# Plain feed-forward blocks with tokens stationary and results turned by DMA, three attention units per layer turned by DMA, and additions placed behind the scaled rows, in a two-layer decoder trunk

## The chip, the cores and the metric

The kernel runs on one core of a Trainium2 chip. The metric is the device time of one execution in microseconds (us), the median of several runs. The profile is one execution recorded by the hardware profiler. Its engines are TensorE (PE; its weight loads are listed apart as PEld), VectorE (DVE), ScalarE (ACT), GpSimd (POOL) and SyncE (SP), which here only issues DMA transfers.

## The reference

The model is a decoder trunk of two layers on 512 tokens of width 1024, all in float32. Each layer is a feed-forward network (2816 hidden columns), a mixing stage with attention and a short convolution side by side, and a second feed-forward network. Cut to what matters here:

```python
def swiglu(h, w_gate, w_up, w_down):
    return (jax.nn.silu(h @ w_gate) * (h @ w_up)) @ w_down
...
    for l in range(DEPTH):
        x = x + 0.5 * swiglu(rms_norm(x, ffn1_norm[l]), ffn1_wg[l], ffn1_wu[l], ffn1_wd[l])

        h = rms_norm(x, mix_norm[l])
        z = h @ w_in[l]
...
        attn_out = sliding_window_attention(q, k, v, attn_sink[l])
        conv_out = short_conv(z[..., V_END:CB_END], z[..., CB_END:CC_END],
                              z[..., CC_END:CH_END], conv_w[l])
        x = x + jnp.concatenate([attn_out, conv_out], axis=-1) @ w_out[l]

        x = x + 0.5 * swiglu(rms_norm(x, ffn2_norm[l]), ffn2_wg[l], ffn2_wu[l], ffn2_wd[l])
    return rms_norm(x, final_norm)
```

Attention has 8 query heads and 2 key-value heads of 64 dimensions, a window of 128 tokens, a linear position bias and a learned sink in the softmax.

## The kernel before

**Numbers in two parts.** Every product is made of three matmuls: each operand is split into a high part (rounded to the fast float type of TensorE) and the low rest, and high x high, low x high and high x low are summed. For a weight tile the high part is a ScalarE cast (`wh`, L205) and the low part a VectorE subtraction (`wl`, L206). `need_raw` loads the raw tile by a DMA from SP's queue (L189) or adds another matrix to it by a DMA from POOL's queue (L200). `take_split` hands a product its tile and has the later ones split ahead. `plan()` fixes the order of all weight tiles, and so the order of the loads on SP and of the casts and subtractions.

**Feed-forward.** Most hidden columns go through blocks that use a seven-product scheme for 2x2 blocks of matrices (`winograd2`, L1081, and `share`, L896, whose matmuls are all in `stream`, L885): tokens are the stationary operand there, 512 weight columns move. Some blocks of 256 hidden columns are "plain", computed directly. The first network of the first layer has two, in another function; the other three networks begin with one, in `plain_halves` (L985). There a weight tile of 128 columns is stationary and the tokens move, in two halves of 256: three tiles in `halves` (L324), the fourth in its own loop (L1010). Since the result has hidden columns on the partitions, it can serve at once as stationary operand of the down-projection. ScalarE applies Silu (L998), VectorE multiplies (L990), and `split` makes the two parts of the result.

**The norm in front.** Class `Norm` sums squares (`sq`, L593) as rows of x are finished; when the four rows of a token half are there, `stage` computes the root (`v`, `r`, `y`) and the scaled rows `xn` (L625). `pull` has TensorE turn two of them (`xt`, L649, eight transposes); casts and subtractions (L658, L659) make the operands `fb` or `hh`. The first half's transposes stand inside the last product of the stage before, the second half's inside the plain block: after 48 and after 60 of its 256-column matmuls. `share(after=norm)` is that stage before in three places (the first network of layer 0 and both output products of the mixing stage). Its accumulators are added to x on VectorE (L924); in its seven steps, `x_m` is step 5 and `z_m`, the last, step 6.

**Turning by DMA, as it is already used.** In `winograd2` the result has tokens on the partitions and must be turned. float32 rows are taken apart into two planes of 16 bits (`apart`, L1098, ScalarE), each plane is sent through a DMA transpose (`send`, L1104, SP's queue), and the turned planes are joined again (`join`, L1158, ScalarE). These steps are put into later blocks by a clock of ticks, two for a weight tile's product.

**Attention.** `mix` (L1360) runs the products with `w_in` and, in between, eight units (4 token blocks x 2 key-value heads; unit number 4g + n). Step by step `attend` (L1499) calls `scores` (matmuls L1435, L1436; exponentials L1456; scaling L1464), `turn` (4 transposes for the first token block, 8 for the others, L1472; casts `ph` L1475, subtractions `pl` L1476) and `values` (L1487, L1488, the product `o`; copy `ol` L1490; addition L1493). The tables SCORES_AT, TURN_AT, VALUES_AT give the steps. Behind each step `go_on` asks for the next weight split.

**Order of work.** A scheduler orders each engine's program; `tc.issue_after(...)` puts an instruction behind a given one in it, and `by_hand` to `by_itself` keeps TensorE's order as written.

## Time and profile before

| | us |
|---|---|
| median of 3 runs | 1652.32 |
| lowest and highest | 1650.25, 1654.33 |
| profiled execution, its own time | 1650.43 |
| span of the profiled execution | 1648.7 |

The granted clock of TensorE is 0.999 of full speed over the span. A row of the chain of waits reads: start, duration, engine, tile, line, number of instructions; a row of a group: busy time and mean duration, then the idle time of the engine just before those instructions and what ended it.

Feed-forward blocks behind norms stand at 502.8 to 527.7, at 828.7 to 853.5 and at 1317.7 to 1342.5 us; attention of layer 0 lies at 375 to 460 us, that of layer 1 some 815 us later. The plain block at 828.7 stands behind a down-projection, the two others behind an output product of the mixing stage.

### The profile page before, as it was taken

Reading aid. Unit: us, or ns where it says so; the run is one execution under the profiler, and the core shown is the slowest. Engines: PE = TensorE matmul, PEld = TensorE weight load, DVE = VectorE, ACT = ScalarE, POOL = GpSimd, SP = SyncE. Lnnn points to the kernel's source line nnn. Section 1 sums busy time; section 2 is a strip of 40 time slices with the busy share of each in tenths; the row PEclk is TensorE's granted clock in tenths of the full one; section 3 lists DMA queues with packets and bytes.
Section 4 is the critical chain, followed back from the end, with each engine's and each line's share of the span. In section 5 each row is a group of like instructions: output and inputs, shape, how many; then the busy total and the mean of one; then the engine's idle time right before and its main releaser. Section 6 shows DMA issues by size and latency. Waiting matters only on the chain.

```text
span 1648.7 us, 21650 instructions
## 1 busy us (share of the span) xinstructions
PE 1637.2 (99%) x7912; PEld 1376.7 (84%) x7912; DVE 1303.5 (79%) x1712; ACT 1089.3 (66%) x1527; POOL 193.0 (12%) x172
## 2 busy tenths in 40 slices
PE   9999999999999999999999999999999999999998
PEld 6888898888889888888898888888988798888886
DVE  7987779867799777798797677896587987767895
ACT  7457777556567567786565777864565765777864
POOL 0011111100111111112001111110002101111111
PEclk9999999999999999999999999999999999999999
DMA  9369999931494778899837889996126946899991
GB/s 256 89 192 225 225 217 257 213 90 52 129 211 108 204 197 212 217 229 251 222 84 185 207 216 220 237 245 189 52 65 155 226 108 168 220 213 231 227 260 71
DMA packets 273791, 303.97 MB, mean 184 GB/s; under 512 B 89332, under 2 KB 157972, under 8 KB 273684
## 3 DMA queue, kind: packets, MB, share of 16 engines
q1 hardware_dynamic: 231156, 223.27, 45.9%
q0 software_dynamic: 41824, 78.65, 28.1%
q8 instruction: 62, 1.02, 0.2%
q10 hardware_dynamic: 704, 0.66, 0.1%
q14 instruction: 45, 0.37, 0.1%
HBM read 263.74 MB, written 2.10 MB: 161 GB/s over the span
## 4 chain that ended last, share of the span: by engine, by line
PE 96%; DVE 2%; ACT 1%; DMA 1%; issue 0%; SPq 0%; ACTq 0%; DVEq 0%
PE x L885 25%; PE y L885 13%; PE x_s L885 10%; PE w L885 6%; PE y_s L885 5%; PE acc L324 5%; PE acc L297 4%; PE acc L298 4%; PE acc L300 4%; PE down L347 3%; PE w_s L885 3%; PE up L1010 1%; PE xt L649 1%; PE y_m L885 1%; PE x_m L885 1%; PE acc L783 1%
## 5 line engine op out<-in xcount | busy, mean ns | idle before, releaser
L206 DVE TENSOR_TENSOR wl<-raw,wh 128x1024 fp32r<-128x1024 f32 (+1 forms) x493 | 599.2, 1220 | 232.2 <-ACT wh L205 231.5
L205 ACT CAST wh<-raw 128x1024 fp32r<-128x1024 f32 (+1 forms) x493 | 512.9, 1044 | 363.8 <-PE acc L298 54.0
L885 PE MATMUL x<-wh,fb 128*128 128x512 f32 x608 | 187.1, 389 | 0.0
L885 PE MATMUL y<-wh,ft 128*128 128x512 f32 x608 | 187.1, 389 | 0.0
L885 PE MATMUL x<-wh,ft 128*128 128x512 f32 x608 | 187.0, 389 | 0.0
L885 PEld LDWEIGHTS x<-wh,ft 128*128 128x128 f32 x608 | 114.1, 188 | 23.7
L885 PEld LDWEIGHTS y<-wh,ft 128*128 128x128 f32 x608 | 114.1, 188 | 23.7
L885 PEld LDWEIGHTS x<-wh,fb 128*128 128x128 f32 x608 | 113.9, 188 | 23.5
L885 PE MATMUL y<-wl,ft 128*128 128x512 f32 x304 | 118.3, 389 | 0.0
L885 PE MATMUL x<-wl,fb 128*128 128x512 f32 x304 | 118.3, 389 | 0.0
L885 PE MATMUL x<-wl,ft 128*128 128x512 f32 x304 | 118.3, 389 | 0.0
L1158 ACT COPY raw_a<-pt 128x1024 uint16<-128x1024 uint16 x76 | 103.3, 1359 | 14.1 <-DMA pt<-pl 14.1
L200 POOL DMA_DIRECT2D raw<-in_ffn_wu_dram x39 | 47.3, 1219 | 544.5 <-DMA raw<-in_ffn_wu_dram 367.8
L297 PE MATMUL acc<-hh,wh 128*128 128x512 f32 x240 | 94.6, 394 | 0.0
L300 PE MATMUL acc<-hh,wl 128*128 128x512 f32 x240 | 93.9, 391 | 0.0
L298 PE MATMUL acc<-hl,wh 128*128 128x512 f32 x240 | 93.6, 390 | 0.0
L885 PE MATMUL w<-wh,fb 128*128 128x512 f32 x304 | 93.5, 389 | 0.0
L885 PE MATMUL x_s<-wh,ft_s 128*128 128x512 f32 x256 | 78.8, 389 | 0.0
L885 PE MATMUL y_s<-wh,ft_s 128*128 128x512 f32 x256 | 78.8, 389 | 0.0
L200 POOL DMA_DIRECT2D raw<-in_ffn_wg_dram x39 | 47.2, 1215 | 236.3 <-DMA raw<-in_ffn_wu_dram 64.6
L885 PE MATMUL x_s<-wh,fb_s 128*128 128x512 f32 x240 | 73.9, 389 | 0.0
L233 DVE TENSOR_TENSOR raw<-raw,raw 128x1024 f32<-128x1024 f32 x58 | 70.5, 1218 | 2.4 <-DMA raw<-in_ffn_wu_dram 1.4
(361 smaller groups left out, 3454.3 us busy)
## 6 DMA issues: line engine op xcount, KB each, us to landing
raw<-in_ffn_wu_dram SPq DMA_DIRECT2D x126, 512.0 KB, 5.0
raw<-in_ffn_wd_dram SPq DMA_DIRECT2D x104, 512.0 KB, 6.7
raw<-in_ffn_wg_dram SPq DMA_DIRECT2D x86, 512.0 KB, 5.2
raw<-in_ffn_wu_dram POOLq DMA_DIRECT2D x39, 512.0 KB, 8.2
raw<-in_ffn_wg_dram POOLq DMA_DIRECT2D x39, 512.0 KB, 6.6
raw<-in_w_in_dram SPq DMA_DIRECT2D x36, 512.0 KB, 4.5
raw<-in_ffn_wd_dram POOLq DMA_DIRECT2D x32, 512.0 KB, 8.2
raw<-raw POOLq DMA_DIRECT2D x20, 512.0 KB, 8.3
```

The lines of the kernel that those rows point to most:

```text
L200: nc.gpsimd.dma_start(out=r, in_=rows_of(*more), accum_op=ALU.add)
L205: cast = nc.scalar.copy(hi, raw)
L206: eng.tensor_sub(lo, raw, f32(hi))
L233: nc.vector.tensor_add(a11, a11, s1)
L297: nc.tensor.matmul(acc, hi[:, k, :], rhs[k][0], start=k == first, stop=False)
L298: nc.tensor.matmul(acc, hi[:, k, :], rhs[k][1], start=False, stop=False)
L300: nc.tensor.matmul(acc, lo[:, k, :], rhs[k][0], start=False, stop=k == last)
L324: nc.tensor.matmul(accs[j][:, t * H : (t + 1) * H], w[:, k, :], x_, start=t + k + i == 0, stop=k == KC - 1 and i == 2, skip_group_check=True,)
L347: nc.tensor.matmul(acc, a[:, k, tok], w[:, k, :], start=i + k + n == 0 and fresh[t], stop=i == last and k == 1 and n == 2, skip_group_chec ...
L649: nc.tensor.transpose(tp[:, j, :], xn[:, j * P : (j + 1) * P], ident)
L885: nc.tensor.matmul(accs[u], x_[:, 2 * h + k, tok], w[:, k, :], start=start and h + k + i == 0, stop=h + k == 2 and i == 2, skip_group_chec ...
L1158: nc.scalar.copy(room.rearrange("p c (n z) -> p c z n", z=2)[:, :, z, :], turned[0][:, NT * z + 2 * c : NT * z + 2 * c + 2, :],)
```

## The change

Three things are changed.

1. **Plain blocks (three, all but those of the first network).** The weight tiles become four tiles of two 128-row chunks with 256 columns of `wg` and 256 of `wu` side by side, each loaded by two DMAs. Tokens are stationary, 512 columns move: per token half, four tiles x two token blocks x six matmuls, 96 in all in place of 192. The second half's norm rows are pulled after the second and third tile. The result is taken apart in four 16-bit copies, turned by two DMA transposes of 1024 columns and joined in four copies at ticks 7 and 8 of the following block; its two parts follow at ticks 9 and 10.
2. **Attention units 1, 3 and 5.** Their scaled probabilities are taken apart (two ScalarE copies of 128x1024), turned by two DMA transposes and joined (two copies) instead of being turned on TensorE (8 transposes each). `ph` and `pl` are made from the joined tile. Their values move to later steps; the tile stays in the pool of raw weights until the join. The other five units stay as they are.
3. **Late additions.** In `share(after=...)` the additions of step 5 stand behind the last scaled row `xn` on VectorE, and in the second half of step 5 the next weight tile's cast stands behind the norm's root on ScalarE, its subtraction behind `xn` on VectorE.

In the built programs SP issues 503 instead of 482 instructions, ScalarE has 51 more and VectorE 6 more.

```diff
@@ -42,8 +42,10 @@
 SCORES_AT = (5, 6, 7, 8, 9, 10, 12, 13)
-TURN_AT = (6, 7, 8, 10, 11, 12, 14, 15)
-VALUES_AT = (7, 8, 9, 11, 12, 13, 15, 16)
+TURN_AT = (6, None, 8, None, 11, None, 14, 15)
+SEND_AT = (None, 7, None, 9, None, 11, None, None)
+JOIN_AT = (None, 10, None, 12, None, 14, None, None)
+VALUES_AT = (7, 11, 9, 13, 12, 15, 15, 16)
@@ -185,6 +188,12 @@
 
     def load(r, n, a, b):
 
+        if n in beside:
+            for i, (src, k0, kc, col, wide) in enumerate(units[n]):
+                state["load"] = nc.sync.dma_start(
+                    r[:, :, i * wide : (i + 1) * wide], rows_of(src, k0, kc, col, wide)
+                )
+            return
         src, k0, _, col, wide = units[n][0]
         state["load"] = nc.sync.dma_start(r[:, a:b, :], rows_of(src, k0 + a, b - a, col, wide))
 
@@ -193,17 +202,17 @@
         while state["raw"] <= min(u, len(units) - 1):
             n = state["raw"]
             _, _, kc, _, wide = units[n][0]
-            r = stock(f"raw_{n}", shape=(P, kc, wide))
+            r = stock(f"raw_{n}", shape=(P, kc, wide * (2 if n in beside else 1)))
             if n >= OPEN:
                 load(r, n, 0, kc)
-            for more in units[n][1:]:
+            for more in () if n in beside else units[n][1:]:
                 nc.gpsimd.dma_start(out=r, in_=rows_of(*more), accum_op=ALU.add)
             raw_of[n] = r
             state["raw"] += 1
 
     def split(hi, lo, raw, eng=nc.vector):
         cast = nc.scalar.copy(hi, raw)
-        eng.tensor_sub(lo, raw, f32(hi))
+        state["sub"] = eng.tensor_sub(lo, raw, f32(hi))
         return cast
 
     def split_far(hi, lo, raw):
@@ -446,8 +455,13 @@
 
         def ffn(wg, wu, wd, stages):
             for what, b in stages:
-                if what == "p":
+                if what == "p" and stages is FIRST:
                     plain(wg, wu, b)
+                elif what == "p":
+                    for k in range(0, KC, 2):
+                        u = add_unit(*((w, k, 2, 2 * b * P, 2 * P) for w in (wg, wu)))
+                        beside.add(u)
+                        order.append((u, None))
@@ -615,14 +629,16 @@
             v, r, y = (small(f"{n}_{i}_{half}", 2) for n in "vry")
             at = 2 * half
             nc.vector.tensor_add(v, self.ss[:, at : at + 2], self.ss[:, NT + at : NT + at + 2])
-            nc.scalar.activation(r, v, AF.Abs_reciprocal_sqrt, scale=1.0 / D, bias=eps)
+            self.guess = nc.scalar.activation(
+                r, v, AF.Abs_reciprocal_sqrt, scale=1.0 / D, bias=eps
+            )
             nc.vector.tensor_scalar(v, v, 1.0 / D, EPS, op0=ALU.mult, op1=ALU.add)
             newton(y, r, v)
             for o in range(2):
                 xns = []
                 for t in (at, at + 1):
                     xns.append(g2(f"xn_{i}_{t}_{o}"))
-                    nc.vector.scalar_tensor_tensor(
+                    self.scaled = nc.vector.scalar_tensor_tensor(
                         xns[-1],
                         xt(t, o),
                         y[:, t - at : t - at + 1],
@@ -893,6 +909,12 @@
             if norm:
                 norm.pull()
 
+    def behind(*those):
+        stack = ExitStack()
+        for one in those:
+            stack.enter_context(tc.issue_after(one.ins))
+        return stack
+
     def share(
         ops, by, between=None, soon=None, after=None, each=lambda: None, w=None, kept=()
     ):
@@ -911,7 +933,11 @@
                 tag = {"x": "mm", "y": "sc", "w": "aux", "z": "mm"}[acc]
                 accs[acc] = [psum(tag, [P, S], f"{acc}_{ops.name}_{m}") for m in range(2)]
             for h in range(2):
-                _, wh, wl = take_split(SPLIT_AHEAD - 1 if after and step in (4, 5) else SPLIT_AHEAD)
+                held_back = after and (step, h) == (5, 1)
+                with behind(after.guess, after.scaled) if held_back else nullcontext():
+                    _, wh, wl = take_split(
+                        SPLIT_AHEAD - 1 if after and step in (4, 5) else SPLIT_AHEAD
+                    )
                 stream(accs[acc], wh, wl, xh, xl, h, start, after if step == 6 else None)
                 each()
                 if soon:
@@ -921,9 +947,10 @@
                 for o, t, sign in shares[step]:
                     for m in range(2):
                         part = xt(2 * t + m, o)
-                        nc.vector.scalar_tensor_tensor(
-                            part, accs[acc][m], by * sign, part, op0=ALU.mult, op1=ALU.add
-                        )
+                        with behind(after.scaled) if after and step == 5 else nullcontext():
+                            nc.vector.scalar_tensor_tensor(
+                                part, accs[acc][m], by * sign, part, op0=ALU.mult, op1=ALU.add
+                            )
                         if after and (step, (o, t)) in ENDS_EARLY:
                             after(2 * t + m, o)
             if not soon:
@@ -984,40 +1011,73 @@
 
         def plain_halves(b):
 
...
-            halves(norm, 3, done)
-            _, hi, lo = take_split()
-            acc = psum("mm", [P, S], f"up_{whole}_{b}")
...
-            up(1, acc)
+            name = f"{whole}_{b}"
+            first = state["group"]
+            held = [take_split(SPLIT_AHEAD - j)[1:] for j in range(4)]
+            room = g8(f"pr_{name}", U16, (P, 4, KC * P))
+            joined = []
+
+            def apart(half, ups):
+                src = ups.rearrange("p t n -> p (t n)").bitcast(U16)
+                src = src.rearrange("p (n z) -> p z n", z=2)
+                with tc.issue_after(state["cast"].ins):
+                    for z in range(2):
+                        nc.scalar.copy(room[:, z, half * S : (half + 1) * S], src[:, z])
+
+            def send(z):
+                with tc.issue_after(load_seen.ins):
+                    nc.sync.dma_start_transpose(
+                        room[:, 2 + z].rearrange("p (g q) -> p g q", q=P), room[:, z]
+                    )
+
+            def join(n):
+                joined.append(g2(f"act_{name}_{n}"))
+                dst = joined[n].bitcast(U16).rearrange("p (t q z) -> p z t q", q=P, z=2)
+                with tc.issue_after(state["cast"].ins):
+                    for z in range(2):
+                        turned = room[:, 2 + z].rearrange("p (t n q) -> p n t q", n=2, q=P)
+                        nc.scalar.copy(dst[:, z], turned[:, n])
+
+            def part(n):
+                if not n:
+                    acts[b] = both(f"a_{name}", shape=(P, 2, 2, S))
+                hi, lo = (a[:, n, :] for a in acts[b])
+                with tc.issue_after(state["cast"].ins):
+                    nc.scalar.copy(hi, joined[n])
+                with tc.issue_after(state["sub"].ins):
+                    nc.vector.tensor_sub(lo, joined[n], f32(hi))
+
+            for half in range(2):
+                load_seen = state["load"]
+                accs = [psum("mm", [P, S], f"up_{name}_{2 * half + t}") for t in range(2)]
+                ups = g2(f"up_{name}_{half}", F32, (P, 2, H))
+                for j, (wh, wl) in enumerate(held):
+                    for t in range(2):
+                        tok = slice(t * P, (t + 1) * P)
+                        for k in range(2):
+                            xh, xl = norm.half(2 * j + k, half)
+                            for i, (x_, w) in enumerate(((xh, wh), (xl, wh), (xh, wl))):
+                                nc.tensor.matmul(
+                                    accs[t],
+                                    x_[:, tok],
+                                    w[:, k, :],
+                                    start=j + k + i == 0,
+                                    stop=j == 3 and k == 1 and i == 2,
+                                )
+                        if j == 3:
+                            nc.scalar.activation(ups[:, t, :], accs[t][:, :H], AF.Silu)
+                            nc.vector.tensor_mul(ups[:, t, :], accs[t][:, H:], ups[:, t, :])
+                    if not half and j in (1, 2):
+                        norm.pull()
+                    if half:
+                        need_split(first + 4 + j)
+                        norm.make(("t2", "t3", "t1", "t4")[j])
+                apart(half, ups)
             by_itself()
-            norm.make("t4")
+            for z in range(2):
+                send(z)
+            for tick, do, n in ((7, join, 0), (8, join, 1), (9, part, 0), (10, part, 1)):
+                pending.setdefault(clock[0] + tick, []).append(lambda do=do, n=n: do(n))
...
+                self.far = JOIN_AT[NT * g + n]
@@ -1462,6 +1523,48 @@
                 for h in range(4):
                     p = self.p[:, h, lo:]
                     nc.vector.tensor_scalar(p, p, sums[:, h : h + 1], None, op0=ALU.mult)
+                if self.far:
+                    self.apart()
+
+            def apart(self):
+
+                if n_of(self) % NT == 1:
+                    self.room = g8(f"pr_{self.name}", U16, (P, 4, KC * P))
+                else:
+                    self.room = xpool.tile(
+                        [P, 4, KC * P], U16, tag="xf", bufs=8, name=f"pr_{self.name}"
+                    )
+                src = self.p.bitcast(U16).rearrange("p h (b k z) -> p z h b k", b=2, z=2)
+                with tc.issue_after(state["cast"].ins):
+                    for z in range(2):
+                        nc.scalar.copy(
+                            self.room[:, z].rearrange("p (b h k) -> p h b k", b=2, h=4), src[:, z]
+                        )
+
+            def send(self):
+                with tc.issue_after(state["load"].ins):
+                    for z in range(2):
+                        nc.sync.dma_start_transpose(
+                            self.room[:, 2 + z].rearrange("p (g q) -> p g q", q=P), self.room[:, z]
+                        )
+
+            def join(self):
+
+                dst = self.p.bitcast(U16).rearrange("p h (k z) -> p z (h k)", z=2)
+                turned = self.p.rearrange("p h k -> p (h k)").rearrange(
+                    "p (b h q) -> p b h q", b=2, h=4
+                )
+                self.pt = []
+                with tc.issue_after(state["cast"].ins):
+                    for z in range(2):
+                        nc.scalar.copy(dst[:, z], self.room[:, 2 + z])
+                for kb in range(2):
+                    hi = g2(f"ph_{self.name}_{kb}", F32R, (P, 4, P))
+                    lo = g2(f"pl_{self.name}_{kb}", F32R, (P, 4, P))
+                    nc.scalar.copy(hi, turned[:, kb])
+                    with tc.issue_after(state["sub"].ins):
+                        nc.vector.tensor_sub(lo, turned[:, kb], f32(hi))
+                    self.pt.append((kb, hi, lo))
 
...
 
         todo = [Unit(n, g) for g in range(NKV) for n in range(NT)]
 
-        def attend(step):
-
+        def n_of(unit):
+            return NT * unit.g + unit.n
+
+        def attend(step, what=(VALUES_AT, TURN_AT, SEND_AT, SCORES_AT)):
+
+            stages = {VALUES_AT: "values", TURN_AT: "turn", SEND_AT: "send", SCORES_AT: "scores"}
             done = None
-            for at, stage in ((VALUES_AT, "values"), (TURN_AT, "turn"), (SCORES_AT, "scores")):
-                if step in at:
-                    done = getattr(todo[at.index(step)], stage)() or done
+            for at in what:
+                for unit, own in zip(todo, at):
+                    if own == step:
+                        done = getattr(unit, stages.get(at, "join"))() or done
             return done
 
...
             step += 1
             with tc.issue_after(last.ins) if last else nullcontext():
                 need_split(state["group"] - 1 + SPLIT_AHEAD)
+            attend(step - 1, (JOIN_AT,))
```

More of the change, by code (lines that the diff above doesn't have):

```diff
@@ L176, in trunk_kernel @@
     raw_of, split_of = {}, {}
+    beside = set()
     state = {"raw": 0, "split": 0, "group": 0, "late": None}
@@ L985, in plain_halves @@
         def plain_halves(b):
-            gates = [g2(f"gate_{whole}_{b}_{j}") for j in range(2)]
-            def up(j, acc):
-                nc.vector.tensor_mul(gates[j], acc, gates[j])
-                if not j:
-                    acts[b] = both(f"a_{whole}_{b}", shape=(P, 2, 2, S))
-                hi, lo = acts[b]
-                split(hi[:, j, :], lo[:, j, :], gates[j])
-            def done(j, acc):
-                if j < 2:
-                    nc.scalar.activation(gates[j], acc, AF.Silu)
-                else:
-                    up(0, acc)
-                norm.make(("t2", "t3", "t1")[j])
@@ L1003, in plain_halves @@
-            halves(norm, 3, done)
-            _, hi, lo = take_split()
-            acc = psum("mm", [P, S], f"up_{whole}_{b}")
-            for t in range(2):
-                for k in range(KC):
-                    xh, xl = norm.half(k, t)
-                    for i, (w, x_) in enumerate(((hi, xh), (hi, xl), (lo, xh))):
-                        nc.tensor.matmul(
-                            acc[:, t * H : (t + 1) * H],
-                            w[:, k, :],
-                            x_,
-                            start=t + k + i == 0,
-                            stop=k == KC - 1 and i == 2,
-                            skip_group_check=True,
-                        )
```

## The prediction

> **What bounds the kernel now.** First the head of the profile's page, then its chain of work that ended last.

> ```profile
> span 1648.7 us, 21650 instructions
> PE 1637.2 (99%) x7912; PEld 1376.7 (84%) x7912; DVE 1303.5 (79%) x1712; ACT 1089.3 (66%) x1527; POOL 193.0 (12%) x172
> ...
> PE 96%; DVE 2%; ACT 1%; DMA 1%; issue 0%; SPq 0%; ACTq 0%; DVEq 0%
> ```

> TensorE is busy in 99% of the span and makes 96% of the chain. So a change gains by taking TensorE work away, or by ending one of its few waits, and it loses wherever it makes TensorE wait. All of TensorE's waits fit in three rows of the view of waits:

> ```profile
> PE xt L649 <- DVE xn L625: 2.1, 3, 0.8
> PE idle L141 <- DVE warm L729: 1.2, 1, 1.2
> PE xt L748 <- DMA x<-in_x_dram: 1.0, 1, 1.0
> ```

> The columns are total us, times, and longest. The last two belong to the start. The first is the only one in mid-kernel: the norm's transposes wait for the scaled rows xn. No weight load appears, so the loads land early enough today. Next, the stretches that the change touches (attention of layer 0; the end of its output product; the plain block; the block behind it), with busy us of PE, PEld, DVE, ACT, POOL, then the granted clock, the DMA share and GB/s:

> ```profile
> 375.00:460.00 85.00, 85.00 (x435) 71.76 (x434) 67.23 (x186) 51.83 (x123) 10.02 (x8) 1.00 0.40 104
> 460.00:502.80 42.80, 41.95 (x191) 34.14 (x190) 40.28 (x52) 31.30 (x45) 6.80 (x6) 1.00 0.91 210
> 502.80:527.70 24.90, 24.90 (x210) 24.88 (x209) 22.56 (x30) 17.46 (x27) 2.41 (x2) 1.00 0.48 113
> 527.70:575.00 47.30, 47.30 (x211) 39.13 (x210) 36.71 (x40) 27.15 (x35) 4.82 (x4) 1.00 0.67 175
> ```

> TensorE is full in all but the second, where it misses 0.85 us; there VectorE has only 2.5 of 42.8 us left. This matters below: the stall lies where VectorE has hardly any slack. The clock is 1.00 throughout, so matmul times can be compared.

> **Part one: the three plain blocks.** The pitch of matmuls comes from the chain, whose columns are start, us and what:

> ```profile
> 502.98 5.75 PE acc L324 x48
> ...
> 521.98 5.76 PE up L1010 x48
> ...
> 544.08 5.44 PE y L885 x24
> ```

> A 256-column matmul takes 5.76/48 = 120 ns and a 512-column one 5.44/24 = 226.7 ns. A block has 144 + 48 = 192 of the first kind, 23.04 us, and becomes 96 of the second kind, 21.76 us: 1.28 us less, three times, -3.8 us. [...]

> What is added runs on ScalarE, and on SP's queue:

> ```profile
> L1098 ACT COPY pl<-u 128x512 uint16<-128x512 uint16 x76 | 42.6, 617 | 17.4 <-DVE u L1142 17.4
> L1158 ACT COPY raw_a<-pt 128x1024 uint16<-128x1024 uint16 x76 | 103.3, 1359 | 14.1 <-DMA pt<-pl 14.1
> L205 ACT CAST a<-gate 128x512 fp32r<-128x512 f32 x10 | 6.1, 622 | 1.0 <-DVE gate L990 0.7 <-DVE gate L962 0.2
> ...
> DMA to landing us min/median/max: 3.2/4.4/8.9
> ```

> Per block: four copies apart at 0.62 = 2.5 us, and four joins of 512 elements at between 0.62 and 1.36/2 = 0.68, about 2.7 us. The casts and subtractions of the result stay two and two. In the block ScalarE has 7.4 us free, in the next one 20 us, and the joins stand seven and eight ticks into the next block, while a transpose lands in at most 8.9 us. I cost this at nothing. The four weight tiles come by eight loads rather than four; the absent load waits above are the cover. If that cover is gone, a tile of 24 matmuls waits for the difference between 5 and 9 us of landing, and the row to look at would be a DMA releaser of wh.

> **Part two: attention.** Units 1, 3 and 5 of eight lose eight transposes each, in two layers 48:

> ```profile
> 441.63 0.87 PE pt L1472 x8
> ```

> At 0.87/8 = 109 ns this is 5.2 us of TensorE. Their price is on ScalarE, in program order behind the weight cast of the step:

> ```profile
> L205 ACT CAST wh<-raw 128x1024 fp32r<-128x1024 f32 x12 | 12.6, 1048 | 19.0 <-PE acc L298 18.8
> L1475 ACT CAST ph<-pt 128x512 fp32r<-128x512 f32 x14 | 7.6, 589 | 0.8 <-PE pt L1472 0.6
> ...
> L1476 DVE TENSOR_TENSOR pl<-pt,ph 128x512 fp32r<-128x512 f32 x28 | 18.2, 686 | 0.6 <-ACT ph L1475 0.4
> ```

> Copies apart of 1024 elements are not in the trace; between twice 0.62 and the join's 1.36 us lies little, but a cast grows by 1048 - 622 = 426 ns from 512 to 1024, so I estimate 1.04 us. A unit costs 2 x 1.04 + 2 x 1.36 = 4.8 us, a layer 14.4 us; ScalarE's 51.8 of 85 us become 66. In sum this fits. What counts is the order: the two joins, two casts ph and the subtraction pl stand between the step's weight cast and the unit's value matmuls, which come one step after the join. Twelve casts in 85 us make a step of 7.1 us. In it a cast waits 19.0/12 = 1.6 us for TensorE to give back its buffer and takes 1.05; then 2.72 + 1.18 + 0.69 = 4.6 us follow. Together 7.25 us: late by about 0.2 us on average, and late by up to 4.6 us if other work (exponentials, copies of o) comes between. Lower end: nothing, if the cast comes early. I take 0.4 us for each of six units, near the sum of the rows: +2.4 us. The net of this part is -2.8 us. The transposes, two for a unit at 1.3 us of SP issue (below), pass the weight loads in a stretch where DMA is busy in only 0.40 of the time, and are sent three steps, 21 us, ahead of their joins:

> ```profile
> L1104 SPq DMA_TRANSPOSE pt<-pl x76: 1242/1308/4877, 125.7 to 1566.5; - x76
> ```

> So loads and landings get no price. Three output weight tiles must wait for joins to release their room; that makes loads later, not uses, as long as ScalarE keeps its step.

> **Part three: late additions.** At the ends of both mixing layers VectorE's order is this:

> ```profile
> 491.74 0.15 DVE L617 TENSOR_TENSOR v<-ss 128x2 f32<-128x2 f32 x1
> ...
> 494.60 0.68 DVE L924 SCALAR_TENSOR_TENSOR x<-x_m,x 128x512 f32<-128x512 f32 x1
> 495.20 0.15 DVE L502 SCALAR_TENSOR_TENSOR y<-v,r 128x2 f32<-128x2 f32 x1
> 495.27 0.68 DVE L924 SCALAR_TENSOR_TENSOR x<-x_m,x 128x512 f32<-128x512 f32 x1
> 495.87 2.73 DVE L625 SCALAR_TENSOR_TENSOR xn<-x,y,gain 128x512 f32<-128x512 f32 x4
> 498.52 0.68 DVE L924 SCALAR_TENSOR_TENSOR x<-x_m,x 128x512 f32<-128x512 f32 x1
> 499.12 1.21 DVE L206 TENSOR_TENSOR wl<-raw,wh 128x1024 fp32r<-128x1024 f32 x1
> 500.25 2.48 DVE L659 TENSOR_TENSOR fb<-xt,fb 128x512 fp32r<-128x512 f32 x4
> 502.65 1.21 DVE L206 TENSOR_TENSOR wl<-raw,wh 128x1024 fp32r<-128x1024 f32 x1
> 503.78 0.68 DVE L924 SCALAR_TENSOR_TENSOR x<-z_m,x 128x512 f32<-128x512 f32 x1
> ```

> The change puts three additions x_m (0.65 us each) and one wl subtraction (1.2) behind xn. At the second half, quoted below, xn follows 1.18 us after v; from 491.74 that gives 492.9 rather than 495.87, some 3 us earlier, and TensorE's wait ends. That wait is, in the timeline of TensorE:

> ```profile
> 496.67 1.32 PE L649 MATMUL xt<-ident,xn 128*128 128x128 f32 x8 [0.84 <-DVE xn L625]
> ...
> 497.75 0.71 PE L885 MATMUL z_m<-wh,fb_m 128*128 128x512 f32 x2
> ```

> Idle before it are 0.84 us, and the eight transposes, 0.87 us of work, take 1.08 until the next matmul starts: 1.05 us lost, at two such sites -2.1 us. The third, behind the first feed-forward block of layer 0, has its additions in the same place; there the wait is bounded by the last subtraction, and I give it nothing.

> But the moved work doesn't vanish. The four rows from 498.52 to 503.78 show VectorE without a gap up to the additions of z_m, and on those hangs the second half of the norm:

> ```profile
> 506.11 0.15 DVE L617 TENSOR_TENSOR v<-ss 128x2 f32<-128x2 f32 x1
> ...
> 507.29 2.74 DVE L625 SCALAR_TENSOR_TENSOR xn<-x,y,gain 128x512 f32<-128x512 f32 x4
> 508.57 1.04 PE L649 MATMUL xt<-ident,xn 128*128 128x128 f32 x8
> ```

> The first two rows of xn are ready at 507.29 + 2 x 0.67 = 508.63; TensorE's transposes start at 508.57. There is no slack. With the earlier stall gone, and 24 matmuls of 226.7 ns (5.44 us) ahead of this point in place of 48 of 120 (5.76), TensorE comes 1.05 + 0.32 = 1.4 us sooner. VectorE has the same pieces to do: 3 us gained, 2.0 + 1.2 given back, and it idles while the norm's root is made. So xn comes between 1.1 us earlier (if the additions of z_m keep up with TensorE) and 1 us later. TensorE waits 0.3 to 2.5 us at each of the two sites. I take 1.8, nearer the upper end since VectorE is full: +3.6 us. The third plain block, behind a down-projection, has the same small slack and only the 0.32 us: +0.3.

> **Sum.** -3.8 - 5.2 - 2.1 + 2.4 + 3.6 + 0.3 = -4.8 us against the profiled execution of 1650.43 us (its span of 1648.7 and 1.7 around it), which stands 1.9 us below the median of the runs shown. 1652.3 - 4.8 = 1647.5.

> **Rivals.**
> *All covers hold.* Attention's joins are in time, and xn keeps up at both sites: -11.1 + 0.6 + 0.3 = -10.2, about 1642 us. For it: ScalarE's free 33 us in the attention stretch, and the early transposes. Against it: VectorE's full stretch.
> *Everything comes back.* Waits replace the work taken away: 0.87 us for each of six units (5.2) and 2.5 at each of two sites: -11.1 + 5.2 + 5.0 + 0.3 = -0.6, about 1651.7 us. For it: VectorE and ScalarE stand one step behind TensorE wherever the work is cut.
> *Slower: ScalarE's order in attention.* ScalarE works strictly in order, so a join that is late holds up the next weight cast, exponentials and o copies too. With attention's waits left out the sum is -7.2 us; so the point is 7.2/6 = 1.2 us of waiting per unit, and over 2.0 it is measurably slower. If half of the 4.6 us behind the cast is exposed at each unit, 6 x 2.3 = 13.8: +6.6, about 1659 us. For it: a step needs 7.25 of 7.1 us on that path. Against it: attention shows no wait of TensorE now, and other casts lie a step ahead.
> *Less work than it says.* The built order shows 96 wide matmuls a block and 48 transposes fewer; only the pitch could differ. If tokens as stationary operand held the 512-column pitch at 240 ns, the blocks would save nothing: 1651.

> **How the numbers follow.** A difference of 0.3%, 5 us, is what a measurement here can tell from none. The forecast case has 0.44, from 1643 to 1651; a little over half of it (0.25) lies beyond 0.3%. All covers hold: 0.20. Everything comes back, with the pitch rival: 0.15. Slower: 0.21. Faster is thus 0.20 + 0.25 = 0.45, same 0.19 + 0.15 = 0.34, slower 0.21. The range goes from 1640, 2 us under the first rival, to 1659, the price of the slower one, whose upper half is left out.

> **What would show it.** Plain blocks: 12 matmuls in 2.72 us where the new line stands, 21.8 us of them in a block. Attention: TensorE busy about 2.6 us less in a layer, and waits of o on ph or pl, 0.4 us in the mean; over 1.2 us and the forecast falls. Norm: the wait of xt on xn in the first half gone, a new one of 1 to 2.5 us at the second-half rows of both sites; if it is absent, the time is nearer 1642. A wait of wh or of a tile on a DMA anywhere in mid-kernel would be a step that I priced at nothing.

## The result and the profile after

The changed kernel takes 1649.76 us (median of 13 runs, 1646.48 to 1652.75) against 1651.61 for the one before: ratio 0.9984, interval 0.9976 to 0.9992. Faster by 1.9 us was measured, 4.8 were forecast. Both lie within the 0.3% that was called no change.

The profiled execution of the change happens to be the slowest of the 13: 1652.75 us, with a span of 1651.0. What it shows need not be in each of the others. In the two profiles SP issues 512 transfers against 482 and ScalarE runs 54 instructions more (1581 against 1527); the 503 and 51 given ahead are too low. The head of its page, its chain, and its waits:

```profile
span 1651.0 us, 21081 instructions
PE 1634.2 (99%) x7576; PEld 1358.5 (82%) x7576; DVE 1299.8 (79%) x1718; ACT 1126.2 (68%) x1581; POOL 193.1 (12%) x172
...
PE 85%; DVE 6%; ACT 4%; DMA 3%; issue 1%; SPq 1%; DVEq 0%; ACTq 0%; POOLq 0%
```

```profile
PE xt L665 <- DVE xn L641: 3.8, 3, 1.7
PE o L1591 <- DVE pl L1566: 1.4, 2, 0.7
PE idle L143 <- DVE warm L745: 1.2, 1, 1.2
PE x L1111 <- ACT p L1095: 1.0, 1, 1.0
PE x_s L901 <- DVE x L951: 0.9, 1, 0.9
```

TensorE has 336 matmuls and transposes fewer, and is still busy for 99% of the span. Its share of the chain fell from 96% to 85% because the chain, followed back from a wait, runs over other engines in stretches where TensorE is at work too (below from 508.70 back to 497.52 us, nearly all on VectorE). The waits on xn are longer than before (3.8 against 2.1 us) and sit elsewhere; waits of o on pl in attention are new. The last two rows stand at 235 and 1104 us, in stretches that the change doesn't touch. The wait on p at 235 us shows in most traces below, with 0.1 to 3.3 us.

The plain block behind layer 0's mixing stage, in the chain of the change (start, us, what):

```profile
497.52 1.20 DVE x L951 x2
498.71 1.61 DVE wl L215 x2
...
507.93 0.77 DVE xn L641
508.70 0.14 issue
508.83 0.64 PE xt L665 x4
509.49 0.63 PE xt L665 x4
510.12 4.34 PE up L1060 x12
514.46 0.87 PE xt L665 x8
515.34 13.62 PE up L1060 x60
```

Sixty matmuls take 13.62 us, 227 ns each, as forecast. But the twelve behind the wait take 4.34 us instead of 2.72. The stretches around them, with the granted clock third from the right (columns as in the prediction), first in layer 0 and then in layer 1:

```profile
503.47:506.88 3.41, 3.41 (x17) 2.71 (x15) 3.41 (x5) 2.17 (x6) 0.06 (x1) 1.00 1.05 244
506.88:510.30 3.42, 1.70 (x12) 1.21 (x11) 2.95 (x9) 1.02 (x3) 0.00 (x0) 1.00 0.99 308
510.30:513.71 3.41, 3.41 (x10) 2.63 (x9) 1.57 (x3) 1.61 (x3) 2.41 (x2) 0.50 0.48 86
1322.67:1326.08 3.41, 1.71 (x12) 1.20 (x11) 2.94 (x9) 1.00 (x3) 0.00 (x0) 1.00 0.99 314
1326.08:1329.50 3.42, 3.42 (x10) 2.64 (x9) 1.59 (x3) 1.63 (x3) 2.41 (x2) 0.50 0.37 77
```

TensorE idles for 1.7 us, starts on xn at 508.83, works at full clock for 1.5 us, and then runs at half its clock for 3.4 us. Layer 1 shows the same. The wait was in the forecast; the halved clock was not.

The times below are read from each trace's matmuls: attention from the first transpose of v to the first `y_m` matmul, the output product from there to the plain block, the plain block to the next one. In us, layer 0 / layer 1, and for blocks the middle one (behind the down-projection) between:

| kernel | attention | output product | plain blocks |
|---|---|---|---|
| before | 97.19 / 97.17 | 30.56 / 30.72 | 24.75 / 24.75 / 24.75 |
| the change | 95.67 / 95.67 | 29.22 / 29.18 | 27.57 / 23.63 / 27.81 |
| e2 blocks alone | 97.19 / 97.23 | 30.49 / 30.64 | 23.73 / 23.55 / 23.67 |
| e3 attention alone | 95.68 / 95.72 | 30.42 / 31.82 | 24.75 / 24.75 / 24.75 |
| e4 additions alone | 97.19 / 97.19 | 29.21 / 29.38 | 26.83 / 24.75 / 26.87 |
| e1 late pull | 95.71 / 95.69 | 29.46 / 29.33 | 23.85 / 23.55 / 23.87 |
| e9 late pull, no additions | 95.67 / 95.67 | 30.55 / 30.71 | 23.55 / 23.55 / 23.55 |
| e5 wait filled | 95.65 / 95.69 | 29.17 / 29.35 | 25.97 / 23.61 / 26.19 |
| e10 wait half filled | 95.69 / 95.73 | 29.17 / 29.45 | 25.97 / 23.63 / 26.24 |
| e6 before, waits of 2.0 to 2.3 | 97.19 / 97.23 | 30.73 / 30.72 | 29.01 / 27.15 / 29.05 |
| e7 before, waits of 0.6 to 0.9 | 97.23 / 97.23 | 30.63 / 30.62 | 26.03 / 25.71 / 26.03 |
| e11 mended | 94.61 / 94.63 | 29.39 / 29.19 | 23.90 / 23.55 / 23.85 |

Attention and output product gain 1.5 us each in each layer; the two blocks behind mixing layers give back 2.8 and 3.1. Against a block without any wait (23.55, in e9) the first of them is 4.0 us longer: 1.7 of idle time, 0.4 because its first eight transposes take 1.3 us and not 0.87, 1.6 of half clock, and 0.3 at its start, which e1 has too.

### The profile page after: what moved, and what is told of

Read it like the earlier page. It is cut to its first block, busy times and chain, and to the rows that moved or that the text cites. A ratio compares the mean times of both kernels' runs of the same rounds, so it can differ in the third digit from the quotient of the medians.

```text
span 1651.0 us, 21081 instructions
## 1 busy us (share of the span) xinstructions
PE 1634.2 (99%) x7576; PEld 1358.5 (82%) x7576; DVE 1299.8 (79%) x1718; ACT 1126.2 (68%) x1581; POOL 193.1 (12%) x172
## 4 chain that ended last, share of the span: by engine, by line
PE 85%; DVE 6%; ACT 4%; DMA 3%; issue 1%; SPq 1%; DVEq 0%; ACTq 0%; POOLq 0%
PE x L901 23%; PE y L901 12%; PE x_s L901 8%; PE w L901 6%; PE y_s L901 4%; PE up L1060 3%; PE down L356 3%; PE acc L306 3%; PE acc L307 3%; PE acc L309 3%; DVE wl L215 2%; PE w_s L901 2%; PE acc L333 2%; DMA raw<-in_ffn_wu_dram 2%; PE x_m L901 1%
## 5 line engine op out<-in xcount | busy, mean ns | idle before, releaser
L1218 ACT COPY raw_a<-pt 128x1024 uint16<-128x1024 uint16 x76 | 103.3, 1359 | 17.1 <-DMA pt<-pl 17.1
L306 PE MATMUL acc<-hh,wh 128*128 128x512 f32 x240 | 94.6, 394 | 0.0
```

The costliest lines, as they stand in the source:

```text
L306: nc.tensor.matmul(acc, hi[:, k, :], rhs[k][0], start=k == first, stop=False)
L1218: nc.scalar.copy(room.rearrange("p c (n z) -> p c z n", z=2)[:, :, z, :], turned[0][:, NT * z + 2 * c : NT * z + 2 * c + 2, :],)
```

## The experiments

Two theories. A: the sum of the prediction is about right, and the halved clock behind the wait takes the rest. B: the clock is incidental, and the rest is late transfers and ScalarE in attention.

**e1, late pull.** The whole change, with one line edited:

```diff
-                    if not half and j in (1, 2):
+                    if not half and j in (2, 3):
                         norm.pull()
```

> The whole change, with the second token half's norm rows pulled after the third and fourth weight tile of a plain block instead of the second and third (2.72 us later). Theory A (wait and clock): the change's own sum of about -4.8 us is right, and what is missing in its median is a halved TensorE clock for some 3 us behind the 1.8 us wait on these rows, at the two sites behind mixing layers, in some of the executions. Then here neither the wait nor the halving is left: about 1643.5 us against 1651.6, ratio 0.995, and runs within 1.5 us of each other. Theory B (the clock is not the cause; the rest is late transfers and ScalarE in attention): only the waits themselves go, twice 1.8 us: about 1646 us, ratio 0.997, and runs as far apart as those of the change (1646.5 to 1652.8).

Measured: 1642.74 us (1642.35 to 1643.68), ratio 0.9943 (0.9929 to 0.9957). Its trace over the times of the change's wait and halved clock:

```profile
506.88:510.30 3.42, 3.42 (x20) 2.87 (x19) 3.00 (x8) 0.31 (x2) 0.00 (x0) 1.00 1.07 332
510.30:513.71 3.41, 3.41 (x21) 2.88 (x20) 1.58 (x3) 3.11 (x5) 2.41 (x2) 1.00 0.33 68
```

No idle time, 21 instructions of TensorE in the second row where the change had 10, clock 1.00. Theory A's number, 1643.5, was met, and the runs lie within 1.3 us. The two causes are still together here: the wait and the clock went at once.

**e5 and e10, the wait filled.** They part the two. Matmuls of zeros stand ahead of the transposes, eight in e5 and four in e10:

```diff
+                    if not half and j == 1 and norm.i % 3 == 2:
+                        spin(8, pairs[1][0])
                     if not half and j in (1, 2):
                         norm.pull()
```

> The whole change, with eight matmuls of zeros (512 columns, some 1.8 us) ahead of the second half's transposes in the two plain blocks behind mixing layers; their result is never read. The rows xn come no sooner. Theory A: TensorE is not idle, so its clock stays: about 1647 us, runs close together, the granted clock 1.00 in the plain block. Theory B: the wait is only filled, the time stays that of the change, about 1649.8, with the same spread; more if the zeros outlast the wait.

> As e5, with four matmuls of zeros rather than eight, so that some 0.9 us of idle time is left ahead of the transposes. In the profiles so far, waits of 1.0 us and less (eight sites) were never followed by a halved clock. If the length of the idle time decides: about 1647 us as e5, granted clock 1.00 in the plain blocks. Rival (any wait at this place does it): 1649.8 as the change.

e5: 1647.11 us (1646.7 to 1651.37, five of seven within 0.7 us), ratio 0.9972 (0.9959 to 0.9984). e10: 1647.69 (1646.88 to 1648.22), 0.9968 (0.9955 to 0.9981). The windows of e5, then of e10, over the place of the wait and over work behind it:

```profile
506.20:508.00 1.80, 1.75 (x8) 0.70 (x8) 1.39 (x6) 0.28 (x1) 0.00 (x0) 1.00 1.08 267
510.40:513.60 3.20, 3.20 (x20) 2.72 (x19) 1.08 (x3) 2.17 (x4) 1.92 (x2) 1.00 0.55 76
```

```profile
506.99:510.40 3.41, 2.57 (x16) 2.05 (x16) 3.41 (x6) 1.22 (x3) 0.48 (x1) 1.00 0.80 296
510.40:513.81 3.41, 3.41 (x21) 2.91 (x20) 1.33 (x3) 2.29 (x5) 1.92 (x2) 1.00 0.56 77
```

xn comes no sooner, and the work between is useless, yet the blocks are 1.6 us shorter than in the change (25.97 against 27.57, 26.19 against 27.81). That is the price of one halving: 3.4 us at half clock. With 0.8 us left idle (e10) it doesn't happen either. Theory B's number, 1649.8, failed in both. Their intervals overlap that of the change (0.9976 to 0.9992), so the times alone wouldn't settle it; the blocks' lengths and the clock do. The profiled executions of e5 and of the change lie 6.0 us apart, and only 3.2 of this is in the two blocks. Most of the rest is in the waits at 235 and 1104 us, which are 2.2 us in the change's profile and 0.3 in e5's. The two longest executions of e5 (1649.51 and 1651.37) have no trace and stay unexplained.

**e6 and e7, the same wait put into the kernel before.** Its second-half rows are pulled 24 matmuls sooner (e6) or 12 (e7):

```diff
-                    if not t and half and j < 2:
+                    if not t and (not half and j if early else half and j < 2):
                         norm.pull()
```

> The kernel before, with the second half's rows pulled 24 matmuls (2.88 us) sooner in its three plain blocks, so that TensorE waits about 2.8 us at each. Theory A: 8.5 us of waits, and behind each a stretch of some 3 us at half the clock in the profile, up to 1.6 us each: 1660 to 1665 us. Theory B (the halving belongs to something else in the change): 1660 us at a granted clock of 1.00 in the plain blocks.

> The same with the rows pulled 12 matmuls (1.44 us) sooner: waits of about 1.4 us at three sites, 4.2 us. Theory A: 1656 us plus 1.6 for each halving that follows, which may be fewer than behind the longer waits; runs far apart. Theory B: 1656 us, granted clock 1.00.

e6: 1660.70 us (1658.76 to 1662.17), ratio 1.0052 (1.0039 to 1.0065); e7: 1656.54 (1655.44 to 1658.46), 1.0027 (1.0017 to 1.0038). In e6 TensorE idles at three blocks, for 2.3, 2.0 and 2.3 us. Its trace, with the wait in the first row of each fence (in the second, in both rows) and the work behind it in the last:

```profile
506.00:509.41 3.41, 1.09 (x10) 0.84 (x9) 2.94 (x9) 0.90 (x4) 0.00 (x0) 1.00 0.81 253
509.41:512.82 3.41, 3.41 (x19) 3.41 (x17) 1.99 (x4) 1.37 (x3) 2.41 (x2) 0.50 0.45 74
```

```profile
833.68:837.09 3.41, 2.42 (x21) 2.22 (x19) 2.42 (x7) 2.55 (x6) 0.70 (x1) 1.00 0.44 144
837.09:840.50 3.41, 2.38 (x19) 2.21 (x20) 3.37 (x7) 1.18 (x2) 0.92 (x2) 1.00 0.87 192
840.50:843.91 3.41, 3.41 (x32) 3.41 (x31) 2.00 (x4) 2.96 (x6) 0.79 (x1) 1.00 1.07 181
```

```profile
1328.61:1332.02 3.41, 1.62 (x13) 1.45 (x14) 3.11 (x8) 1.08 (x3) 0.47 (x1) 1.00 0.75 246
1332.02:1335.43 3.41, 3.41 (x18) 3.41 (x18) 1.47 (x4) 1.56 (x4) 1.94 (x2) 0.50 0.56 82
```

Two of three are halved. The middle one, with a wait of 2.0 us, is not, and its block is longer by 2.4 us (27.15 - 24.75) against 4.3: its wait and 0.4 of slower transposes. So nothing in the new blocks is needed for it; the old kernel does the same with a wait of 2.3 us. The time of e6 lies at the lower end of theory A's range and next to theory B's number, so it doesn't part them; the clock does. No stretch of e7, with waits of 0.6 to 0.9 us, was halved. Without a halving both theories forecast 1656 us, so its time doesn't part them either.

Theory A holds, with a limit that it hadn't named: the length of the wait alone doesn't decide. The traces show what went with a halving. In the three with half clock in mid-kernel, its changes lie whole multiples of 3.413 us apart. Those of the change, at 510.30, 513.71, 1326.08 and 1329.50 us, are 1, 238 and 1 such steps apart; those of e6 (509.4, 512.8, 1332.0 and 1335.4) 1, 240 and 1; those of e8 (238.3 and 245.2) 2. The fall of the clock behind the last matmul lies on the same steps, 333, 336 and 411 of them after the first change. So a trace can be cut into steps of this length, as in the rows above; in a trace without a halving they are counted back from that last fall. Between 20 and 1630 us, the eleven traces that were read in windows of 1 us (all but e9's and e11's) have some 5170 steps at full clock. In five of them TensorE was busy for 0.32 to 0.50 of the step, and half clock followed each time: two in the change, two in e6, one in e8. In all others it was busy for 0.70 or more, and half clock followed none. The middle wait of e6 falls on the border of two steps and leaves each busy for 0.7. A wait of 1.7 us, as in the change, makes a step half idle only if it lies wholly within it. Where the steps lie differs from trace to trace (the first begins 1.7 us after the program's start in the change and 0.8 in e6, counted modulo 3.4), so whether an execution is halved looks to be in part chance. This last step is the author's estimate and no run shows it; the change has a trace of one execution alone.

This fits the executions of the change: the four quickest (1646.5 to 1647.2) were granted 0.999 of the clock in the mean, the two slowest (1652.2 and 1652.8) 0.996 and 0.997. It isn't the only source of scatter, though. The kernel before, without these waits, has executions from 1650.25 to 1655.64 us in the same comparison, and none of the longer ones has a trace.

**e2, e3 and e4, one part each.** Edits: the tables of attention and the placing of additions set back (e2), the blocks and the placing (e3), the blocks and the tables (e4).

> The plain blocks alone. By the prediction's steps -3.8 us of matmuls and 0.3 us of wait at each of three blocks: about 1648.7 us, ratio 0.998. Rival (all comes back through the wait on the second half's rows, which TensorE now reaches sooner): no change, 1651.6.

> The attention units alone. By the trace of the change, 5.2 us of transposes less and one wait of 0.84 us on pl in each layer: -3.5 us, about 1648.1 us, ratio 0.998. By the prediction's term, -2.8: 1648.8. Rival (ScalarE's order takes it all back, or delays other things): 1651.6 or more.

> The late additions alone. The wait of 1.05 us on the first half's rows goes at two sites; by the prediction's steps the second half's rows come about 0.6 us later there while TensorE comes 1.05 us sooner, so a wait of some 1.6 us takes its place: net +0.6 at each site, 1652.8 us against 1651.7, and in theory A up to 1.6 us more in executions in which the halved clock follows. Rival (the second half's rows come sooner as well): -2.1, about 1649.6 us.

e2: 1648.77 us, ratio 0.9980 (0.9971 to 0.9988). This is the number of the prediction's steps. Its table row shows a gain of 1.0 to 1.2 us per block. Of the 0.3 us of extra wait that was charged to each block, the two behind mixing layers show 0.1 to 0.2 and the middle one nothing.

e3: 1650.37 us, 0.9989 (0.9980 to 0.9998), a smaller gain than either number. Attention itself took 1.5 us less in each layer, 3.0 in all, as priced. In the profiled execution 1.1 us of it is lost in the output product of layer 1, where a weight cast came late:

```profile
PE o L1558 <- DVE pl L1533: 1.3, 2, 0.7
PE y_m L901 <- ACT wh L214: 1.3, 1, 1.3
```

In the chain, that cast leads back over ScalarE's and VectorE's work to an 8.8 us transfer of `w_out`. Whether the joins, which hold the room of three of these tiles, make such transfers later was not tried; this wait is at most 0.5 us in the other kernels with the same attention (e8), and the kernel before has none.

e4: 1653.36 us, 1.0009 (1.0000 to 1.0018): the forecast 1652.8 rather than the rival's 1649.6. Each output product gains 1.35 us, and the block behind it loses 2.1, with waits of 0.7 us on fb and 0.5 on xn in its trace. Alone, the additions make the kernel no faster.

**e9, the additions once nothing waits behind them.** e1, with e4's edit left out.

> The late pull of e1 without the late additions: only blocks and attention. If the additions are worth something once nothing waits behind them, their stage (output product of the mixing layer) goes from 29.4 back to 30.6 us in both layers while the plain blocks stay at 23.9: 1642.7 + 2.5 = about 1645.2 us. Rival (they only moved the wait, as in e4): the time of e1, 1642.7.

Measured: 1644.16 us (1643.50 to 1645.63), ratio 0.9948 (0.9935 to 0.9961), between the two numbers. By the table the output products lose 1.1 and 1.4 us and the blocks win back 0.3 each. In e1 the additions are thus worth some 1.9 us by the traces. By the ratios it is 0.0005, or 0.8 us, well within both intervals, so the times don't show it.

**e8 and e11, two more waits addressed.** e1 with

```diff
-VALUES_AT = (7, 11, 9, 13, 12, 15, 15, 16)
+VALUES_AT = (7, 11, 9, 13, 12, 16, 15, 16)
...
-                    if not t and half and j < 2:
+                    if not t and half and j:
                         norm.pull()
```

> The late pull of e1, with two more waits of its trace addressed: the fifth of the changed attention units' values come one step later (wait of 0.84 us on pl, in two layers), and in the first product of the mixing layers the second half's rows are pulled one weight tile (12 matmuls of 256 columns, 1.44 us) later (wait of 0.83 us at 345 us). If both waits simply go: 1642.7 - 1.7 - 0.8 = 1640.2 us. Rival (they come back as later waits, on the copies of o or on the low parts): 1642.7 or more.

> The kernel of e8 once more, beside e9, since its profile had a wait of 3.3 us at 235 us in a part that no kernel here changes. If that wait comes by chance: about 1640 us, below e1, its attention stage at 94.6 us against 95.7. Rival (the moved values or pull bring it about): 1643 us again, with the long wait at 235 us in the profile.

e8: 1643.09 us (1638.92 to 1645.70), 0.9942 (0.9928 to 0.9956), the number of its rival, though both waits are gone. e11, the same kernel: 1639.93 (1638.97 to 1641.78), 0.9923 (0.9908 to 0.9937), the number forecast. In e8's profiled execution, the slowest of its six, the wait at 235 us took 3.3 us, to 239.4, and the longest halving in mid-kernel began before it ended:

```profile
234.91:238.33 3.42, 1.22 (x11) 1.01 (x9) 2.61 (x4) 3.00 (x6) 0.00 (x0) 1.00 0.96 226
238.33:241.74 3.41, 2.34 (x11) 2.34 (x12) 2.86 (x4) 3.41 (x8) 1.20 (x1) 0.50 1.08 203
241.74:245.15 3.41, 3.41 (x18) 3.41 (x18) 1.53 (x3) 1.92 (x4) 0.00 (x0) 0.50 1.02 137
```

In e11 the view of waits has for TensorE only that of the start and one of 0.3 us:

```profile
PE idle L143 <- DVE warm L745: 1.2, 1, 1.2
PE x_s L901 <- DVE wl L215: 0.3, 1, 0.3
```

The kernel beats the one before by 9.1 us in e8 and by 11.5 in e11; the median of its twelve executions is 1640.6 us. That it also beats e1 (1642.74) rests on e11 and on the traces: attention takes 94.6 us in place of 95.7. The wait at 235 us varies between executions of one kernel (3.3 us in e8, 0.1 in e11); what makes it long was not tried.

## Why the prediction came out as it did

The direction, the time (1647.5 against 1649.76, inside the range) and most terms held; the size of the gain, -4.8 against -1.9 us, did not. The size of a TensorE wait was the weak term, and a halved clock behind it wasn't in the sum at all.

- *Matmuls of the blocks, -1.28 us each.* -1.20 where undisturbed (24.75 to 23.55). Right.
- *Attention, -2.8 us.* -3.0. The price was right (2.2 us of the 5.2 came back, 2.4 forecast), the place was not: one unit per layer waits, not three (twice 0.7 us idle), and for VectorE's subtraction pl behind a wl, not for ScalarE. With that unit's values one step later (e11) attention is shorter by the full 2.6 us per layer. ScalarE's row rose to 64.2 of 85 us (66 forecast), the copies apart took 1.04 us as estimated, the joins 1.35.
- *Transposes and loads, nothing.* The new transposes landed in 3.1 to 3.3 us, and no wait on them appears.
- *First half's wait, -1.05 at each site.* -1.3 and -1.5.
- *Second half's wait, 1.8 us at each site.* The idle time was 1.7 us, but without the halving the blocks of e5 are 2.4 and 2.6 us longer than an undisturbed one (25.97 and 26.19 against 23.55): slower transposes and the block's start were left out. The cause was right. In layer 0 the second half's first xn comes 35.9 to 36.1 us after the output product's first matmul in every kernel with the late additions (the change, e1, e4, e5, e8, e10, e11), and 34.9 to 35.0 us in those without (the kernel before, e2, e3, e9). So it is the additions that delay it, by about 1 us, the upper end of the prediction's range. The middle block's +0.3 was 0.1.
- *What failed* is the price of that wait: 1.8 us were charged as idle time and no more. Behind it TensorE ran at half clock in the profiled execution, which cost another 1.6 us at each site; the mean clocks of the other executions point to halvings in some of them and not in all. The prediction had read the clock as 1.00 throughout before and took it as given for the changed kernel. Without the halving the gain is 4.6 us (e5) or 3.7 (e10), and their rows of the table add up to 4.3 and 4.0. That the forecast sum of 4.8 lies so near is in part luck: the second half's waits cost 1.5 us more than charged, and ending the first half's gave 0.6 to 0.8 more than counted. The time came nearer than the gain because the kernel before took 1651.61 us here and not the 1652.3 from which the forecast started.
- *Rivals.* All covers hold (1642) is e1 in effect, but only with the pull moved. ScalarE's order in attention did not decide anything. Everything comes back (1651.7) was nearer to the measured time than the forecast; its 2.5 us at each site is what the wait costs without the halving, but its 5.2 us in attention were 2.2.

The change lost its gain inside itself: it moved the rows of the first half forward, TensorE's arrival at the second half forward too and the second half's xn back, and left the place of the second pull where it was. One tile later, 7 us were there. An estimate from e2 and e3: blocks and attention without the additions would gain 3.3 + 3.0 = 6.3 us by the table, more than the change with them; that kernel was not run.

## What to carry to other kernels

Where TensorE is made faster ahead of a fixed meeting point with another engine, move the meeting point too. Price a new wait by its length and by the clock behind it: here a wait of 1.7 us was followed by another 1.6 us of loss, and filling it with useless matmuls gave that part back. When executions of one kernel scatter, compare their mean granted clocks, and look in a trace for a stretch of lower clock, before looking for late transfers.
